# Encoder layer on one core: token-major projections with weights taken 512 columns at a time instead of 256

## The chip, the cores and the metric

The kernel runs on 1 core of one Trainium2 chip. The metric is the device time of one execution in microseconds (us); before the change it is 2485.04 us, the median of 3 runs (2484.7 to 2485.36).

## The reference, cut to what matters

One encoder layer is applied to two independent streams: a prompt of 1024 tokens and a sample of 512 tokens, each with a memory of 256 tokens, width 1024, everything float32.

```python
def encoder_layer(x, mem, p):
    u = rmsnorm(x, p['mix_norm_g']) @ p['w_in']
    ssd_out = ssd_mixer(u[..., OFF_Z:OFF_XBC], u[..., OFF_XBC:OFF_DT], u[..., OFF_DT:OFF_Q], ...)
    att_out = attention_mixer(u[..., OFF_Q:OFF_K], u[..., OFF_K:OFF_V], u[..., OFF_V:IN_COLS], ...)
    h = x + jnp.concatenate([ssd_out, att_out], axis=-1).astype(x.dtype) @ p['w_out']
    h = h + memory_cross_attention(rmsnorm(h, p['xatt_norm_g']), rmsnorm(mem, p['mem_norm_g']), ...)
    hm = rmsnorm(h, p['mlp_norm_g'])
    return h + jnp.square(jax.nn.relu(hm @ p['mlp_w1'])) @ p['mlp_w2']
```

`w_in` gives in turn the gates (512 columns), the convolved channels (1024), the step sizes (16), queries, keys and values (512 each). The memory projection `xatt_wkv` has 2048 columns, `w_out` 1024.

## The kernel before, in words

**Products.** A float32 product is made of three float32r products: operand = high part + low part, and `mm3` (lines 198 to 201) adds high x high, high x low and low x high in one PSUM bank. `load_w` (line 179) brings 1 MB of weights: four DMAs of 256 KB into `raw` (4 buffers), four ScalarE casts to `whi` (line 189), four subtractions to `wlo` (line 191), in turns on GpSimd and VectorE. `whi` and `wlo` have three buffers each.

**Token-major projections.** Gates, queries, keys, values, memory keys and values, and the output projection are computed with a tile of 128 tokens stationary and weights moving. `slab` takes 256 columns of all 1024 rows; `proj` (line 273) makes 24 products of 256 columns for one token tile into one of three `mm` banks:

```python
        for k in range(KT):
            mm3(ps, hi[:, k, ts], lo[:, k, ts], wh[:, k, :], wl[:, k, :], k == 0, k == KT - 1)
```

What reads the bank: for gates a tanh on ScalarE and a product on VectorE (lines 381, 382); for queries and keys a ScalarE copy (line 511), then `heads` (norm and rotation on ScalarE, VectorE and GpSimd) and, one pair of tiles later, `transposed`; for memory keys a copy and a square (lines 896, 898), and right behind them scaling (line 910) and TensorE transposes (line 912); for memory values a copy, a cast on VectorE (line 901) and a subtraction on GpSimd (line 902); for the output projection an addition to the residual on VectorE (line 958).

**Other dense work.** `xbc` (the convolved channels) and the feed-forward (`mlp`) already move 512 columns per product; the cross-attention queries move 256 and stay so.

**The order.** Every dense part is a generator that yields after about 3 us of TensorE work. `weave` advances the mixers (`ssd`, the scan, and `att`, the dilated attention, first of the sample, then of the prompt) by a rate of steps per yield, and side work (norms and transposes of tokens) by another. A tile scheduler then fixes each engine's order when the program is built; engines run their orders strictly and wait on semaphores. In time the program runs: sample `w_in` (0 to 91 us), its gates (to 111), its queries, keys, values (to 197), prompt gates (to 256), prompt `xbc` (to 380), prompt queries, keys, values (to 572), memory (to 725), sample output projection (to 790), sample cross-attention (to 960), sample feed-forward (to 1415), prompt output projection (to 1515), prompt cross-attention (to 1760), prompt feed-forward (to the end).

Of the kernel before, what the change touches and what calls it, by code (L numbers as in the profile page):

```python
# [84 lines left out]
def encoder(ctx: ExitStack, tc: tile.TileContext, I, y_p, y_s):  # L85
# [186 lines left out]
    def proj(w, quads, t):  # L272
# [6 lines left out]
        return ps  # L279

# [19 lines left out]
    def w_in(st, pool, wx, first=False):  # L300
# [67 lines left out]
        def gates(b):  # L368
            for c in range(2):
                if b == 0:  # L370
                    wz.append(slab(W_IN, OFF_Z + c * 256))
                yield from gate(c, wz[c], range(b * 4, b * 4 + 4, 2))

        def gate(c, w, ts):
            for t in ts:
                th = pool.tile([128, 512], F32, name="ev").rearrange("p (t c) -> p t c", t=2)
                for i in range(2):
                    if i:
                        yield
                    ps = proj(w, at, t + i)  # L380
                    nc.scalar.activation(th[:, i], ps, AF.Tanh, scale=0.5)
                    nc.vector.scalar_tensor_tensor(th[:, i], th[:, i], 1.0, ps, op0=OP.add, op1=OP.mult)  # L382
                dst = st.zs[t * 128:t * 128 + 256, c * 256:c * 256 + 256]
                nc.sync.dma_start(dst.rearrange("(t p) c -> p t c", p=128), th)
                catch_up()
                yield
# [64 lines left out]
    def w_in_qkv(st, pool, rot, mid=None):  # L451
# [7 lines left out]
        def heads(c, t, hl):  # L459

            qk = c // 2
            e, sq = f(hl[1]).rearrange("p (t c) -> p t c", t=2), f(hl[0])
            x = e.rearrange("p t (h e) -> p t h e", h=4)
            x3 = e.rearrange("p t (h e) -> p (t h) e", h=4)
            nc.scalar.activation(sq, e.rearrange("p t c -> p (t c)"), AF.Square)
# [3 lines left out]
            nc.vector.tensor_tensor(x3, x3, r[:, :8, None].to_broadcast([128, 8, 64]), op=OP.mult)  # L469
            t1, t2 = x[..., 0:8], x[..., 8:16]  # L470
            m = sq[:, 0:256].rearrange("p (j t h c) -> p j t h c", j=4, t=2, h=4)
            for j, src in enumerate((t1, t2, t1, t2)):
                w = rot[qk][:, t:t + 2, j, None, :].to_broadcast([128, 2, 4, 8])
# [4 lines left out]
        def transposed(c, t, hl):  # L478
            qk = c // 2
            e = f(hl[1]).rearrange("p (t c) -> p t c", t=2)  # L480
            pt = tp_bank()
            for hp in range(2):
                for i in range(2):
                    o = (hp * 2 + i) * 128
                    nc.tensor.transpose(pt[:, o:o + 128], e[:, i, hp * 128:hp * 128 + 128], perm)
# [3 lines left out]
            for j in range(2):  # L489
                dst = st.qk[qk, (c % 2) * 2:(c % 2) * 2 + 2, j, :, t * 128:t * 128 + 256]  # L490
                nc.sync.dma_start(dst.rearrange("h p t -> p h t"), f(hl[j]).rearrange("p (h t) -> p h t", h=2))
# [3 lines left out]
        order = [(c, t) for c in range(4) for t in range(0, nt, 2)]  # L495
        order += [(c, b * 4 + t) for b in range(nt // 4) for c in (4, 5) for t in (0, 2)]
        ws = {}
        for c, t in order:
            if c not in ws:
                ws[c] = slab(W_IN, OFF_Q + c * 256)  # L500
            w = ws[c]
            if mid and (c, t) == (4, 4):
                mid()
            if True:
                hl = [pool.tile([128, 512], F32R, name="ev") for _ in range(2 if c < 4 else 1)]
                e = f(hl[-1]).rearrange("p (t c) -> p t c", t=2)
                for i in range(2):
                    if i:
                        yield
                    ps = proj(w, st.at, t + i)  # L510
                    nc.scalar.copy(e[:, i], ps)
                if behind:
                    transposed(*behind.pop())
                if c < 4:
                    heads(c, t, hl)
                    behind.append((c, t, hl))
                else:
                    for i in range(2):
# [4 lines left out]
                yield  # L523
# [359 lines left out]
    def memory(pool, late=None):  # L883
        for c in range(8):
            w = slab(WKV, c * 256)
            if late and c == 4:
                late()
            for st in (S, R):
                need("mem" + st.tag)
                kf = pool.tile([128, 512], F32, name="ev").rearrange("p (m c) -> p m c", m=2)  # L890
                ss = pool.tile([128, 2], F32, name="kss", bufs=2)
                for mt in range(2):
                    if mt:
                        yield
                    ps = proj(w, st.mt[:1], st.mt[1] + mt)
                    nc.scalar.copy(kf[:, mt], ps)
                    if c < 4:
                        nc.scalar.activation(ps, ps, AF.Square, accum_out=ss[:, mt:mt + 1])
                hl = [pool.tile([128, 2, 256], F32R, name="ev") for _ in range(2)]
                if c >= 4:  # L900
                    nc.vector.tensor_copy(hl[0], kf)
                    nc.gpsimd.tensor_tensor(hl[1], kf, f(hl[0]), op=OP.subtract)
                    for j in range(2):
                        nc.sync.dma_start(st.v[:, c - 4, j], f(hl[j]).rearrange("p m c -> p (m c)"))
                    yield
                    continue
                r = rstd(pool, ss, 2, 256)
                pt = tp_bank().rearrange("p (e m) -> p e m", e=2)
                for mt in range(2):
                    nc.vector.tensor_scalar(kf[:, mt], kf[:, mt], r[:, mt:mt + 1], None, op0=OP.mult)  # L910
                    for e in range(2):
                        nc.tensor.transpose(pt[:, e, mt * 128:mt * 128 + 128], kf[:, mt, e * 128:e * 128 + 128], ident)
# [347 lines left out]
```

## Time and profile before

| | |
|---|---|
| median of 3 runs | 2485.04 us |
| the profiled execution | 2483.99 us |
| its span (first to last instruction) | 2481.9 us |
| TensorE products busy | 2413.2 us, 97% of the span, 14435 |
| VectorE, ScalarE, GpSimd busy | 57%, 39%, 30% |
| granted TensorE clock, mean | 0.986 |
| DMA | 272.28 MB, 35.2% of 16 engines |

TensorE products overlap in the pipeline and their ends are modelled, so the busy share says only that the engine seldom stands still. What one product costs is read from the distance between the starts of two that follow each other. A wait is shown in brackets in the timeline: how long the engine stood, and what released it.

### The profile page before, as it was taken

What the parts mean: (1) busy time and instruction counts of PE and PEld (TensorE: products, weight loads), DVE (VectorE), ACT (ScalarE), POOL (GpSimd) and SP (SyncE); (2) the same over time, 40 slices, a digit from 0 to 9 for tenths busy, and PEclk for the clock granted to TensorE, in tenths of its full rate; (3) what the DMA queues carried; (4) which work ended last, traced back from release to release, by engine and by line L of the source; (5) the groups of instructions that cost most, each with busy time, mean ns of one, the idle gap of its engine ahead of it and who ended that gap; (6) DMA issues with size and microseconds to landing.
All of it is one profiled execution on the core that took longest, in us unless ns stands there. A gap on an engine that the chain in (4) does not pass through costs nothing.

```text
span 2481.9 us, 38736 instructions
## 1 busy us (share of the span) xinstructions
PE 2413.2 (97%) x14435; PEld 2129.5 (86%) x14435; DVE 1416.4 (57%) x2870; ACT 977.0 (39%) x2393; POOL 749.0 (30%) x612
## 2 busy tenths in 40 slices
PE   8899999999899998999999999999999999999999
PEld 6899789998798997888888899999888888888887
DVE  7676876658866566565655636555634434444344
ACT  6445455545544555444433325333521211212111
POOL 3253313425654212332424212111222222322221
PEclk9999999999899999999999999999999999999999
DMA  5555344547675344335335511111111111111111
GB/s 182 182 191 172 121 138 144 169 135 256 226 256 161 87 124 117 105 107 134 107 95 179 181 45 50 54 52 52 35 44 42 52 52 34 54 49 51 51 34 68
DMA packets 258603, 272.28 MB, mean 110 GB/s; under 512 B 43474, under 2 KB 222960, under 8 KB 258416
## 3 DMA queue, kind: packets, MB, share of 16 engines
q1 hardware_dynamic: 258416, 269.82, 35.2%
q8 instruction: 114, 1.87, 0.3%
q14 instruction: 73, 0.60, 0.1%
HBM read 215.55 MB, written 54.20 MB: 109 GB/s over the span
## 4 chain that ended last, share of the span: by engine, by line
PE 73%; DMA 3%; DVE 3%; issue 1%; ACT 1%; POOL 1%; SPq 0%; ACTq 0%; POOLq 0%; DVEq 0%
PE mm L199 15%; PE mm L201 14%; PE mm L200 14%; PE tp L199 7%; PE tp L200 7%; PE tp L201 7%; PE mc L800 2%; PE ma L771 1%; PE mb L787 1%; PE tp L218 1%; DMA se<-acp 1%; DVE se L626 1%; PE mc L635 0%; DMA ak<-qkp 0%; PE tp L981 0%
## 5 line engine op out<-in xcount | busy, mean ns | idle before, releaser
L191 POOL TENSOR_TENSOR wlo<-raw,whi 128x512 fp32r<-128x512 f32 x240 | 364.9, 1537 | 550.3 <-ACT whi L189 451.2
L199 PE MATMUL mm<-whi,chi 128*128 128x256 f32 x1792 | 521.1, 292 | 2.3 <-DVE ev L382 1.7
L201 PE MATMUL mm<-whi,clo 128*128 128x256 f32 x1792 | 511.6, 288 | 1.3 <-DVE clo L225 1.2
L200 PE MATMUL mm<-wlo,chi 128*128 128x256 f32 x1792 | 511.6, 286 | 0.0
L1112 DVE TENSOR_TENSOR h<-mm,h 128x512 f32<-128x512 f32 x384 | 262.5, 688 | 380.7 <-PE mm L201 380.4
L191 DVE TENSOR_TENSOR wlo<-raw,whi 128x512 fp32r<-128x512 f32 x240 | 296.7, 1250 | 97.1 <-ACT whi L189 96.2
L199 PEld LDWEIGHTS mm<-whi,chi 128*128 128x128 f32 x1792 | 344.6, 192 | 5.0 <-DVE ev L382 2.4
L189 ACT CAST whi<-raw 128x512 fp32r<-128x512 f32 x480 | 265.2, 618 | 203.8 <-PE tp L200 100.3
L200 PEld LDWEIGHTS mm<-wlo,chi 128*128 128x128 f32 x1792 | 344.3, 192 | 0.8
L201 PEld LDWEIGHTS mm<-whi,clo 128*128 128x128 f32 x1792 | 342.2, 192 | 2.3 <-DVE clo L225 2.2
L199 PE MATMUL mm<-whi,hidh 128*128 128x512 f32 x768 | 304.2, 396 | 0.0
L201 PE MATMUL mm<-whi,hidl 128*128 128x512 f32 x768 | 303.1, 395 | 0.0
L200 PE MATMUL mm<-wlo,hidh 128*128 128x512 f32 x768 | 302.6, 394 | 0.0
L200 PE MATMUL tp<-clo,whi 128*128 128x512 f32 x720 | 284.4, 395 | 0.0
L199 PE MATMUL tp<-chi,whi 128*128 128x512 f32 x720 | 284.3, 395 | 0.0
L201 PE MATMUL tp<-chi,wlo 128*128 128x512 f32 x720 | 284.0, 394 | 0.0
L1096 POOL TENSOR_TENSOR hidl<-hr,hidh 128x512 fp32r<-128x512 f32 x96 | 124.6, 1298 | 475.7 <-ACT hidh L1095 302.6
L1095 ACT CAST hidh<-hr 128x512 fp32r<-128x512 f32 x96 | 59.6, 621 | 401.1 <-PE mm L200 325.7
L201 PEld LDWEIGHTS mm<-whi,hidl 128*128 128x128 f32 x768 | 144.4, 188 | 33.6
L200 PEld LDWEIGHTS mm<-wlo,hidh 128*128 128x128 f32 x768 | 144.6, 188 | 32.3
L199 PEld LDWEIGHTS mm<-whi,hidh 128*128 128x128 f32 x768 | 144.5, 188 | 32.2
L201 PEld LDWEIGHTS tp<-chi,wlo 128*128 128x128 f32 x720 | 135.4, 188 | 31.1
(284 smaller groups left out, 4132.7 us busy)
## 6 DMA issues: line engine op xcount, KB each, us to landing
raw<-in_mlp_w_dram SPq DMA_DIRECT2D x256, 256.0 KB
raw<-in_w_in_dram SPq DMA_DIRECT2D x96, 256.0 KB
qkp<-ev SPq DMA_DIRECT2D x32, 256.0 KB
raw<-in_xatt_wkv_dram SPq DMA_DIRECT2D x32, 256.0 KB
se<-acp SPq DMA_DIRECT2D x16, 512.0 KB
raw<-in_w_out_dram SPq DMA_DIRECT2D x32, 256.0 KB
raw<-in_xatt_wq_dram SPq DMA_DIRECT2D x32, 256.0 KB
ak<-qkp SPq DMA_DIRECT2D x32, 256.0 KB
```

The source lines that it names most:

```text
L189: nc.scalar.copy(hi[:, sl, sc], raw)
L191: eng.tensor_tensor(lo[:, sl, sc], raw, f(hi[:, sl, sc]), op=OP.subtract)
L199: nc.tensor.matmul(ps, lh, rh, start=start, stop=False)
L200: nc.tensor.matmul(ps, lh, rl, start=False, stop=False)
L201: nc.tensor.matmul(ps, ll, rh, start=False, stop=stop)
L218: nc.tensor.transpose(pt[:, k, t, :], xn[t][:, (2 * kp + k) * 128:(2 * kp + k + 1) * 128], units(2 * kp + k))
L626: nc.vector.scalar_tensor_tensor(w[:, h], cbm[:, 0, g], col[2], w[:, h], op0=OP.mult, op1=OP.add)
L771: nc.tensor.matmul(pq[:, i, :W], qu, ops[i][0][j], start=j == 0, stop=j == 1)
L800: nc.tensor.matmul(po[:, i * 64:i * 64 + 64], pT[:, i * nk + j, :], ops[i][1][j][:, rs], start=j == 0, stop=j == nk - 1)
L1095: nc.scalar.copy(hh[:, ft], r)
L1096: nc.gpsimd.tensor_tensor(hl[:, ft], r, f(hh[:, ft]), op=OP.subtract)
L1112: nc.vector.tensor_tensor(h[t][:, cs], ps, h[t][:, cs], op=OP.add)
```

## The change

Weights of the token-major projections come as two halves of 512 rows with 512 columns each (`wide_slab`), 1 MB per half, so one wide slab holds two of the three weight buffers. `wide_proj` takes token tiles in pairs with a bank each: both tiles on one half, then both on the other, and the next pair begins with the half used last. What reads a bank now reads 512 columns at once; memory keys are finished one head later through a list `behind`; memory values lose the copy on ScalarE and VectorE's cast (a ScalarE cast and a VectorE subtraction straight from the bank remain), and GpSimd's subtraction goes. DMA rows change with it: weights 2 KB instead of 1 KB, gates and values 2 KB instead of 1 KB, queries and keys 512 bytes instead of 1 KB. The rates of `weave` change too. A yield still stands for about the same work: 12 products of 512 columns instead of 24 of 256.

```diff
+        r, c = {8: (2, 256), 4: (1, 512), 2: (2, 256)}[a]
         for s in range(4):
-            raw = wp.tile([128, 2, 256], F32, name="raw", bufs=4)
-            sl = slice(s * 2, s * 2 + 2) if a == 8 else slice(0, 2)
-            sc = slice(0, 256) if a == 8 else slice(s * 256, s * 256 + 256)
+            raw = wp.tile([128, 512], F32, name="raw", bufs=4).rearrange("p (r c) -> p r c", r=r)
+            sl = slice(s * r, s * r + r) if a > 2 else slice(0, 2)
+            sc = slice(0, c) if a > 2 else slice(s * c, s * c + c)
...
+    def wide_slab(w, c0):
+        src = w[:, c0:c0 + 512].rearrange("(u k p) c -> u p k c", p=128, k=4)
+        return [load_w(src[u], 4, 512) for u in range(2)], [0]
...
+    def wide_proj(w, quads, tiles, each):
+        halves, last = w
+        for t0 in tiles[::2]:
+            ps = [mm_bank() for _ in range(2)]
+            for n in range(2):
+                u = last[0] if n == 0 else 1 - last[0]
+                wh, wl = halves[u]
+                for i in range(2):
+                    hi, lo = quads[(t0 + i) // 4]
+                    ts = slice((t0 + i) % 4 * 128, (t0 + i) % 4 * 128 + 128)
+                    for k in range(4):
+                        kk = u * 4 + k
+                        mm3(ps[i], hi[:, kk, ts], lo[:, kk, ts], wh[:, k, :], wl[:, k, :],
+                            n == 0 and k == 0, n == 1 and k == 3)
+                    if n == 1:
+                        each(t0 + i, ps[i])
+                    yield
+            last[0] = 1 - last[0]
...
+            if b == 0:
+                wz.append(wide_slab(W_IN, OFF_Z))
+            yield from wide_proj(wz[0], at, range(b * 4, b * 4 + 4), gate)
+        def gate(t, ps):
+            th = pool.tile([128, 512], F32, name="ev")
+            nc.scalar.activation(th, ps, AF.Tanh, scale=0.5)
+            nc.vector.scalar_tensor_tensor(th, th, 1.0, ps, op0=OP.add, op1=OP.mult)
+            nc.sync.dma_start(st.zs[t * 128:t * 128 + 128, :], th)
+            catch_up()
...
+        def query_key(qk):
+            def each(t, ps):
+                hl = [pool.tile([128, 512], F32R, name="ev") for _ in range(2)]
+                nc.scalar.copy(f(hl[1]), ps)
                 if behind:
                     transposed(*behind.pop())
-                if c < 4:
-                    heads(c, t, hl)
-                    behind.append((c, t, hl))
-                else:
-                    for i in range(2):
-                        for g in range(2):
-                            r0 = 64 + (t + i) * 128 + g * 64
-                            dst = st.vd[r0:r0 + 64, (c - 4) * 256:(c - 3) * 256]
-                            nc.sync.dma_start(dst.rearrange("(r j) c -> j r c", r=4), e[g * 64:g * 64 + 64, i, :])
-                yield
+                heads(qk, t, hl)
+                behind.append((qk, t, hl))
+            return each
+        def value(t, ps):
+            e = pool.tile([128, 512], F32, name="ev")
+            nc.scalar.copy(e, ps)
+            if behind:
+                transposed(*behind.pop())
+            for g in range(2):
+                r0 = 64 + t * 128 + g * 64
+                dst = st.vd[r0:r0 + 64, :]
...
+        for part, each in enumerate((query_key(0), query_key(1), value)):
+            w = wide_slab(W_IN, OFF_Q + part * 512)
+            for b in range(nt // 4):
+                if mid and part == 2 and b == 1:
+                    mid()
+                yield from wide_proj(w, st.at, range(b * 4, b * 4 + 4), each)
...
+        def values(st, c, t, ps):
+            hl = [pool.tile([128, 512], F32R, name="ev") for _ in range(2)]
+            nc.scalar.copy(hl[0], ps)
+            nc.vector.tensor_tensor(hl[1], ps, f(hl[0]), op=OP.subtract)
+            for j in range(2):
+                dst = st.v[:, c:c + 2, j, t % 2 * 256:t % 2 * 256 + 256]
+                nc.sync.dma_start(dst, f(hl[j]).rearrange("p (h c) -> p h c", h=2))
+        behind = []
+        for c in range(4):
...
+                        behind.extend(held)
+                    for _ in range(len(behind) - 1):
+                        keys(*behind.pop(0))
+                yield from wide_proj(w, st.mt[:1], range(st.mt[1], st.mt[1] + 2), each)
...
+        def each(t, ps):
+            hs = st.h[t][:, cs]
             nc.vector.tensor_tensor(hs, ps, hs, op=OP.add)
-            if c == 3 and t % 2:
+            if cs.start and t % 2:
                 done(t // 2)
-            yield
+        for c in range(2):
+            w = wide_slab(W_OUT, c * 512)
+            cs = slice(c * 512, c * 512 + 512)
+            for pr in range(st.nt // 2):
+                need("mix%d%s" % (pr, st.tag))
+                yield from wide_proj(w, st.mixT, range(pr * 2, pr * 2 + 2), each)
...
-        weave(mixing, 0.3, marked(w_in_qkv(S, pool, rot), "qkv s"))
+        weave(mixing, 0.4, marked(w_in_qkv(S, pool, rot), "qkv s"))
-        weave(mixing, 0.45, marked(w_in(R, pool, wx), "w_in p"), 1.0)
+        weave(mixing, 0.5, marked(w_in(R, pool, wx), "w_in p"), 1.0)
-        weave(mixing, 0.9, marked(w_in_qkv(R, pool, rot, memories), "qkv p"), 1.0)
+        weave(mixing, 1.0, marked(w_in_qkv(R, pool, rot, memories), "qkv p"), 1.0)
-        weave(mixing, 0.6, chain(S, (atA,), hp, tp_only), 2.0)
+        weave(mixing, 0.7, chain(S, (atA,), hp, tp_only), 2.0)
-            weave(mixing, 0.65, mlp(S, hid, ready))
+            weave(mixing, 0.5, mlp(S, hid, ready))
```

The change also moves instructions. **TensorE, sample gates and queries:** `ma<-sxs,sbt` is the scan's first state update (line 582 before, 594 after); `mm<-w..,chi/clo` are gate and query products. Before:

```order
L201 MATMUL mm<-whi,clo 128x256
L549 MATMUL ma<-ident,sacs 64x128
L582 MATMUL ma<-sxs,sbt 128x256 x2
L199 MATMUL mm<-whi,chi 128x256
L200 MATMUL mm<-wlo,chi 128x256
```

Now:

```order
L206 MATMUL mm<-wlo,chi 128x512
L207 MATMUL mm<-whi,clo 128x512
L594 MATMUL ma<-sxs,sbt 128x256 x2
L205 MATMUL mm<-whi,chi 128x512
L206 MATMUL mm<-wlo,chi 128x512
```

Before, the update stands behind the third of the eight gate projections (72 of 192 products); now it stands behind all 96 wide gate products and the first 96 wide products of the queries.

**TensorE, end of the prompt gates:** `tp<-ident,xn` transposes normalised tokens of the second block of the prompt, `mc`, `mb`, `ma` belong to the scan. Before:

```order
L201 MATMUL mm<-whi,clo 128x256
L635 MATMUL mc<-sx,se 128x64 x4
L199 MATMUL mm<-whi,chi 128x256
L200 MATMUL mm<-wlo,chi 128x256
L199 MATMUL mm<-whi,chi 128x256
L200 MATMUL mm<-wlo,chi 128x256
L201 MATMUL mm<-whi,clo 128x256 x2
L635 MATMUL mc<-sx,se 128x64 x2
L199 MATMUL mm<-whi,chi 128x256
L200 MATMUL mm<-wlo,chi 128x256
L199 MATMUL mm<-whi,chi 128x256
L200 MATMUL mm<-wlo,chi 128x256
```

Now:

```order
L594 MATMUL ma<-sxs,sbt 128x256
L224 MATMUL tp<-ident,xn 128x128 x2
L594 MATMUL ma<-sxs,sbt 128x256
L647 MATMUL mc<-sx,se 128x64 x5
L224 MATMUL tp<-ident,xn 128x128 x6
L647 MATMUL mc<-sx,se 128x64 x3
L619 MATMUL mb<-sbc 128x128 x2
L656 MATMUL ma<-carry,sbc 128x256 x2
L656 MATMUL mb<-spb,sbc 128x256 x2
L224 MATMUL tp<-ident,xn 128x128 x8
L594 MATMUL ma<-sxs,sbt 128x256 x2
L205 MATMUL mm<-whi,chi 128x512
```

Before, gate products stand between the small ones; now 34 small instructions follow each other with no gate product between them.

## Rows read from the trace of the kernel before

**Rows 1.** The page: engines' busy time, and the TensorE clock in 40 slices.

```profile
PE 2413.2 (97%) x14435; PEld 2129.5 (86%) x14435; DVE 1416.4 (57%) x2870; ACT 977.0 (39%) x2393; POOL 749.0 (30%) x612
...
PEclk9999999999899999999999999999999999999999
```

**Rows 2.** Busy time by stretch, the page's engines in columns, clock, DMA.

```profile
core 0: us, PE busy (x) PEld busy (x) DVE busy (x) ACT busy (x) POOL busy (x), PEclk, DMA share, GB/s
...
91.00:111.00 20.00, 20.00 (x144) 20.00 (x145) 10.46 (x19) 9.66 (x23) 6.19 (x6) 0.85 0.72 231
...
572.00:725.00 153.00, 138.27 (x1015) 131.85 (x1014) 124.25 (x242) 84.75 (x246) 91.86 (x74) 0.93 0.70 231
...
1850.00:2400.00 550.00, 550.00 (x2370) 445.40 (x2369) 223.92 (x295) 110.75 (x196) 142.08 (x98) 1.00 0.15 48
```

**Rows 3.** Groups by line and shape: busy us, mean ns, idle before.

```profile
L199 PE MATMUL mm<-whi,chi 128*128 128x256 f32 x1792 | 521.1, 292 | 2.3 <-DVE ev L382 1.7 <-ACT chi L224 0.4
L200 PE MATMUL mm<-wlo,chi 128*128 128x256 f32 x1792 | 511.6, 286 | 0.0
```

**Rows 4.** Timeline of TensorE, prompt memory values: start, duration.

```profile
694.38 0.28 PE L201 MATMUL mm<-whi,clo 128*128 128x256 f32 x1
...
696.52 0.29 PE L201 MATMUL mm<-whi,clo 128*128 128x256 f32 x1
```

**Rows 5.** Timeline of TensorE, sample gates.

```profile
87.20 2.04 PE L582 MATMUL ma<-sxs,sbt 128*128 128x256 f32 x4 [5.32 <-DMA sbt<-bts]
90.97 0.58 PE L199 MATMUL mm<-whi,chi 128*128 128x256 f32 x1 [1.73 <-DVE ev L382]
91.36 0.42 PE L200 MATMUL mm<-wlo,chi 128*128 128x256 f32 x1
...
96.69 0.41 PE L201 MATMUL mm<-whi,clo 128*128 128x256 f32 x1
...
97.98 0.28 PE L201 MATMUL mm<-whi,clo 128*128 128x256 f32 x1
```

**Rows 6.** Waits of TensorE: total us, times, longest.

```profile
PE mc L635 <- POOL se L628: 9.7, 4, 4.3
PE tp L218 <- DVE xn L239: 8.9, 7, 4.5
PE tp L218 <- DVE clo L225: 8.6, 3, 3.4
...
PE tp L912 <- DVE ev L910: 3.0, 3, 1.1
```

**Rows 7.** Timeline, one slab made in the memory stage.

```profile
637.28 2.18 ACT L189 CAST whi<-raw 128x512 fp32r<-128x512 f32 x4 [2.58 <-PE mm L201]
638.46 3.06 DVE L191 TENSOR_TENSOR wlo<-raw,whi 128x512 fp32r<-128x512 f32 x2 [1.45 <-ACT whi L189]
```

**Rows 8.** Timeline, a slab made where the output projection begins.

```profile
723.80 0.28 PE L201 MATMUL mm<-whi,clo 128*128 128x256 f32 x1
730.55 2.18 ACT L189 CAST whi<-raw 128x512 fp32r<-128x512 f32 x4
...
736.89 1.27 POOL L191 TENSOR_TENSOR wlo<-raw,whi 128x512 fp32r<-128x512 f32 x1
```

**Rows 9.** Groups by line and shape: what reads the banks.

```profile
L1112 DVE TENSOR_TENSOR h<-mm,h 128x512 f32<-128x512 f32 x384 | 262.5, 688 | 380.7 <-PE mm L201 380.4
...
L511 ACT COPY ev<-mm 128x256 f32<-128x256 f32 x72 | 26.0, 368 | 41.6 <-PE mm L201 36.0 <-DMA qks<-ev 3.3 <-DMA vds<-ev 2.0
L958 DVE TENSOR_TENSOR h<-mm,h 128x256 f32<-128x256 f32 x48 | 20.0, 421 | 38.1 <-PE mm L201 38.0
...
L336 ACT COPY xr<-mm 128x512 f32<-128x512 f32 x24 | 13.9, 580 | 19.6 <-PE mm L201 15.0 <-DVE cacc L348 4.6
L902 POOL TENSOR_TENSOR ev<-ev 128x512 fp32r<-128x512 f32 x8 | 11.8, 1481 | 11.5 <-DVE ev L901 8.5 <-issue 2.3 <-POOL wlo L191 0.7
```

More of the change, by code (lines that the diff above doesn't have):

```diff
@@ L489, in transposed @@
             for j in range(2):
-                dst = st.qk[qk, (c % 2) * 2:(c % 2) * 2 + 2, j, :, t * 128:t * 128 + 256]
-                nc.sync.dma_start(dst.rearrange("h p t -> p h t"), f(hl[j]).rearrange("p (h t) -> p h t", h=2))
+                dst = st.qk[qk, :, j, :, t * 128:t * 128 + 128]
+                nc.sync.dma_start(dst.rearrange("h p t -> p h t"), f(hl[j]).rearrange("p (h t) -> p h t", h=4))
         behind = []
-        order = [(c, t) for c in range(4) for t in range(0, nt, 2)]
@@ L496, in w_in_qkv @@
[L496 to L511, printed above, removed]
+        def query_key(qk):
+            def each(t, ps):
+                hl = [pool.tile([128, 512], F32R, name="ev") for _ in range(2)]
+                nc.scalar.copy(f(hl[1]), ps)
@@ L523, in w_in_qkv @@
-                yield
+                heads(qk, t, hl)
[9 more added lines that the diff above has]
+                dst = st.vd[r0:r0 + 64, :]
+                nc.sync.dma_start(dst.rearrange("(r j) c -> j r c", r=4), e[g * 64:g * 64 + 64, :])
@@ L883, in memory, with keys @@
     def memory(pool, late=None):
-        for c in range(8):
-            w = slab(WKV, c * 256)
-            if late and c == 4:
+        def keys(st, c, kf, ss):
+            hl = [pool.tile([128, 2, 256], F32R, name="ev") for _ in range(2)]
+            r = rstd(pool, ss, 2, 256)
+            pt = tp_bank().rearrange("p (e m) -> p e m", e=2)
+            for mt in range(2):
+                nc.vector.tensor_scalar(kf[:, mt], kf[:, mt], r[:, mt:mt + 1], None, op0=OP.mult)
+                for e in range(2):
+                    nc.tensor.transpose(pt[:, e, mt * 128:mt * 128 + 128], kf[:, mt, e * 128:e * 128 + 128], ident)
+            for e in range(2):
+                g = gqk[:, e:e + 1]
+                nc.scalar.activation(hl[0][:, e], pt[:, e], AF.Identity, scale=g)
+                nc.vector.scalar_tensor_tensor(hl[1][:, e], pt[:, e], g, f(hl[0][:, e]), op0=OP.mult, op1=OP.subtract)
+            for j in range(2):
+                nc.sync.dma_start(st.kt[:, c, j], f(hl[j]).rearrange("p e m -> p (e m)"))
+        def values(st, c, t, ps):
+            hl = [pool.tile([128, 512], F32R, name="ev") for _ in range(2)]
+            nc.scalar.copy(hl[0], ps)
+            nc.vector.tensor_tensor(hl[1], ps, f(hl[0]), op=OP.subtract)
+            for j in range(2):
+                dst = st.v[:, c:c + 2, j, t % 2 * 256:t % 2 * 256 + 256]
+                nc.sync.dma_start(dst, f(hl[j]).rearrange("p (h c) -> p h c", h=2))
+        behind = []
+        for c in range(4):
+            w = wide_slab(WKV, c * 512)
+            if late and c == 2:
                 late()
@@ L899, in memory @@
[L899 to L908, printed above, removed]
@@ L917, in memory @@
-                for j in range(2):
-                    nc.sync.dma_start(st.kt[:, c, j], f(hl[j]).rearrange("p e m -> p (e m)"))
-                yield
+                held = []
+                def each(t, ps):
+                    if c > 1:
+                        if behind:
+                            keys(*behind.pop(0))
+                        return values(st, c * 2 - 4, t, ps)
+                    mt = t % 2
+                    for h in range(2):
+                        if mt == 0:
+                            kf = pool.tile([128, 512], F32, name="ev").rearrange("p (m c) -> p m c", m=2)
+                            held.append((st, c * 2 + h, kf, pool.tile([128, 2], F32, name="kss", bufs=6)))
+                        _, _, kf, ss = held[h]
+                        cs = slice(h * 256, h * 256 + 256)
+                        nc.scalar.copy(kf[:, mt], ps[:, cs])
+                        nc.scalar.activation(ps[:, cs], ps[:, cs], AF.Square, accum_out=ss[:, mt:mt + 1])
+                    if mt:
+                        behind.extend(held)
+                    for _ in range(len(behind) - 1):
+                        keys(*behind.pop(0))
@@ L946, in w_out, with each @@
             st.h.append(x)
-        ws = {}
-        order = [(c, t) for c in range(2) for t in range(st.nt)]
-        order += [(c, pr * 2 + t) for pr in range(st.nt // 2) for c in (2, 3) for t in range(2)]
-        for c, t in order:
-            if c not in ws:
-                ws[c] = slab(W_OUT, c * 256)
-            if c == 0 and t % 2 == 0:
-                need("mix%d%s" % (t // 2, st.tag))
-            ps = proj(ws[c], st.mixT, t)
-            hs = st.h[t][:, c * 256:c * 256 + 256]
+        def each(t, ps):
+            hs = st.h[t][:, cs]
             nc.vector.tensor_tensor(hs, ps, hs, op=OP.add)
-            if c == 3 and t % 2:
+            if cs.start and t % 2:
                 done(t // 2)
-            yield
+        for c in range(2):
[4 more added lines that the diff above has]
+                yield from wide_proj(w, st.mixT, range(pr * 2, pr * 2 + 2), each)
     def xattn(st, xk, xp, bank, done):
```

58 lines of the change are left out of this document (11 added, 47 removed).

## The prediction

> **What bounds the kernel now.** I read first the page's engine rows: TensorE is busy for 97% of the span, no other engine for more than 57% [rows 1]. The reader should see that time is to be won or lost only on TensorE's own line: in the distance between its products, in its waits, and in its clock. That share says nothing of distance, because products overlap: one of 256 columns is shown as 292 ns long [rows 3] while the next starts 0.119 us later [rows 4]. So the second view is the timeline: from 694.38 to 696.52 lie 18 steps, 2.14 us / 18 = 0.119 us per product of 256 columns [rows 4]. For 512 columns I use the stretch 1850 to 2400, where the prompt's feed-forward moves only 512-column products and TensorE never stands: 550 us / 2370 = 0.232 us [rows 2]. The third view is the list of TensorE's waits: some ten us each for four kinds [rows 6], all in the first 970 us, where scan, attention and norms run beside the projections. The fourth is the clock: it falls in a few slices only [rows 1], and the timeline shows when: after a wait of 5.3 and one of 1.7 us, products start 0.213 us apart for 25 steps (91.36 to 96.69), half clock (1.2 GHz), before 0.12 comes back [rows 5]. In the windows the memory stage is the worst: TensorE idle for 14.7 of 153 us at clock 0.93, VectorE busy for 124.25 [rows 2].
>
> **The change part by part.** The sum is made against the profiled execution's 2483.99 us; the median of the runs is 1.05 us above it.
>
> *Fewer, wider products.* 5376 products of 256 columns run on lines 199 to 201 (1792 on each, [rows 3]); the cross-attention queries keep 1152 of them (4 slabs x 12 tiles x 24). The other 4224 become 2112 of 512 columns. Each pair cost 2 x 0.119 = 0.238 us and becomes 0.232 us [rows 2, 4]: 0.0057 us x 2112 = 12.0 us off. All of it is on TensorE's line. Bounds: one stretch of 18 steps is read to about 0.01 us, so 0.1194 is as possible, which makes 14 us; and at half clock, where 256 columns take 0.213 [rows 5], no row shows 512 columns, so nothing is counted there. I take 12, bounds 5 and 17. The Trainium skill, "TensorE: Matmul & The Clock Gate", section "Back-to-back issue gap", speaks against a gain of this size: it gives a lone gap of N/2.4 + 2.5 ns, so that a merged pair saves only 2.5 ns, an estimate of 5.3 us for 2112. The rows are above its gaps at both widths (119 against 109, 232 against 216), and the measurement decides.
>
> *The scan's first update in the sample's gates.* Before, it stands behind the third gate projection and waits 5.32 us for a load; VectorE, standing behind the same update, then reads a gate bank late, another 1.73 us; 25 products follow at half clock, 25 x (0.213 - 0.119) = 2.4 us [rows 4, 5]. Together 9.4 us. Now it stands behind all 96 wide gate products and 96 of the queries, 192 x 0.232 = 44.5 us after the gates begin, where before it stood 72 x 0.119 = 8.6 us after: 36 us later, against a load that came 5.3 us late. I take all 9.4; bounds 0 (another wait comes there) and 9.4.
>
> *The cluster at the end of the prompt's gates.* Now 34 small instructions of scan and norm follow each other without gate products between. They are chained through VectorE, ScalarE and GpSimd, as the scan's and the norm's known waits are [rows 6]. The nearest price is a wait of the norm for VectorE's low part, 8.6 us in 3 times, 2.9 each, plus half clock as in [rows 5], 2.4: I take 5. Bounds 0 and 12 (the longest norm wait, 4.5, and the longest scan wait, 4.3 [rows 6], with half clock after).
>
> *Memory keys one head later.* Their transposes waited 3.0 us in 3 times for the scaling [rows 6]; with a head's delay I take 2 off, bounds 0 and 3.
>
> *Halves of weights.* A second half finds its buffer only when the previous slab's half is left. From there to its first use lie at least the second tile's other half (12 products) and the next pair on the first half (24): 36 x 0.232 = 8.4 us, where a whole spare slab stood before. How long does making a slab take after the release? 4.2 us in the memory stage: ScalarE stood ready and cast at 637.28, VectorE ended at 641.52 [rows 7]. At the output projection's start 14.1 us: the last product that read the buffer ended at 724.08, the casts began at 730.55 and GpSimd ended at 738.16 [rows 8]. So a wait is between 0 and 5.7 us. Most stages are like the first, so I take 2 us in all. Queued behind such casts on ScalarE are copies out of banks; TensorE needs the first of those banks again only 24 products later.
>
> *Priced at nothing.* Bank readers: VectorE's 48 additions of 421 ns become 24 of 688, ScalarE's 72 copies of 368 ns become 36 of 580 [rows 9]; both lie beside TensorE's work, and would cost only where these engines are late already. GpSimd loses 8 x 1.48 us of memory values [rows 9]; the 9.7 us that TensorE waited for GpSimd [rows 6] could shrink by it, but the removed work stands later than those waits, so: nothing, bound 9.7 off. Banks: a pair holds two of three; from the end of its first tile to the need of that bank lie 24 wide products, 5.6 us, as before two projections, 5.7. DMA: the same bytes, in longer rows for weights and shorter for queries and keys; its share is 0.70 at most in these stages [rows 2]. Rates: a yield stands for the same work, so 0.1 more only moves scan and attention forward, out of the sample's feed-forward; their products cost the same there. The cover is VectorE's idle time, least in the memory stage (28.75 of 153 us, [rows 2]), whose rate stays.
>
> Sum: -12.0 - 9.4 + 5 - 2 + 2 = -16.4 us; 2483.99 - 16.4 = 2467.6, and with the 1.05 us of the median 2469 rounded.
>
> **The rivals.**
> *Paid back (no change).* Wide products save only some 2.5 ns per pair, the wait at the sample's gates goes, and the prompt's cluster (12) and halves (6) take the place: -5 - 9.4 + 12 - 2 + 2 = -2.4 to 2483. For it: that scheduled orders always leave some such waits, and that the fixed part of 5.7 ns is a small difference of two readings. Against it: 2370 products agree on 0.232. The skill's gap from above would make the first term 5.3 instead of 12.
>
> *Memory loosens (larger gain).* Its scan no longer waits for GpSimd (9.7 and 3.0 us, [rows 6]), with half clock after them (clock 0.93 of 153 us is 21 us at half speed, 10.7 lost, [rows 2]): 20 of these come off: 2449. For: 11.8 us less on GpSimd. Against: VectorE is busy for 81% there, and stays so.
>
> *Halves late (slower).* In the built order eight of the sixteen second halves have only 8 to 13 us of products between release and first use (at 0.232 us each), 10.4 on average. If making one takes 14.1 us [rows 8] in all of these, they wait 8 x 3.7 = 30 us together, and some five of them long enough for half clock as in [rows 5], 12 us more: 2469 - 2 + 42 = 2509. It decides from about 12 us per half on, where the gain is gone. For: VectorE and GpSimd carry the subtractions and are busiest in these stages. Against: [rows 7], and the four casts wait at the head of ScalarE's queue as they do now.
>
> That the change doesn't do what it says is excluded: the built order has 2112 products of 512 columns where 4224 of 256 stood.
>
> **How the numbers follow.** About 0.2% (5 us) is what a measurement of this kernel can tell from no change. Forecast 0.63 (2455 to 2480), paid back 0.13, memory loosens 0.13, halves late 0.11. Faster takes forecast and memory: 0.76; same 0.13; slower 0.11. The range leaves out halves late and the far half of memory loosens: 2447 to 2489; its ends are also the bounds of the terms (-17 - 9.4 - 9.7 - 3 = -39 below, -5 + 12 + 6 - 9.4 = +4 above).
>
> **What would show it.** Right: products on 512 columns start 0.232 us apart in gates, queries, keys, values, memory and output projection; no wait for `sbt` around 85 us and full clock through the sample's gates; prompt gates longer by some us with a wait of the norm or scan there. Waits for `whi` or `wlo` at 8 us or less of products would show the halves. Wrong: a distance of 0.238 or more, or more waits in memory and output projection than before, or a change of the sample feed-forward's length by more than the attention steps it loses.

## The result, and the profile after

The changed kernel takes 2456.31 us, the median of 4 runs (2454.34 to 2459.82), beside 2485.2 us for the kernel before: ratio 0.9886, 95% interval 0.9868 to 0.9903. It is faster by 28.9 us, inside the range on record and 12.7 us below the number forecast. The profiled execution took 2455.78 us with a span of 2454.0.

The page of the kernel after, engines and TensorE clock:

```profile
PE 2393.4 (98%) x12323; PEld 2005.8 (82%) x12323; DVE 1410.0 (57%) x2834; ACT 967.3 (39%) x2337; POOL 736.3 (30%) x604
...
PEclk9999999999989999999999999999999999999999
```

Against [rows 1] there are 2112 TensorE products fewer; one slice of 40 is under nine tenths of full clock in either, and the mean granted clock is 0.993 (0.986 before). The other engines do nearly the same work. The groups by shape, then a piece of the timeline inside the sample's gates:

```profile
L205 PE MATMUL mm<-whi,chi 128*128 128x512 f32 x704 | 288.2, 409 | 8.8 <-ACT chi L230 5.6 <-ACT ev L513 2.3 <-ACT mm L942 0.8
...
L205 PE MATMUL mm<-whi,chi 128*128 128x256 f32 x384 | 108.9, 285 | 0.0
```

```profile
85.06 0.40 PE L207 MATMUL mm<-whi,clo 128*128 128x512 f32 x1
...
89.23 0.39 PE L207 MATMUL mm<-whi,clo 128*128 128x512 f32 x1
89.47 0.53 PE L549 MATMUL mb<-sa,tab 128*128 128x32 f32 x4
89.83 0.41 PE L550 MATMUL mb<-sa,one 128*128 128x64 f32 x2
90.05 0.48 PE L205 MATMUL mm<-whi,chi 128*128 128x512 f32 x1
```

From 85.06 to 89.23 lie 18 steps: 4.17 / 18 = 0.232 us, the distance forecast. There is no idle time in brackets where [rows 5] had 5.32 and 1.73 us. TensorE's longest kinds of waits over the whole span, after its wait for the program's first load:

```profile
PE mm L205 <- ACT chi L230: 5.6, 3, 2.7
PE ma L656 <- DVE carry L601: 5.2, 3, 3.8
PE tp L224 <- DVE clo L231: 4.7, 2, 3.3
PE mc L647 <- POOL se L640: 4.7, 4, 2.3
...
PE tp L903 <- DVE ev L901: 2.0, 3, 0.8
```

Against [rows 6], the waits for GpSimd's `se` fell from 9.7 to 4.7 us and the memory keys' wait from 3.0 to 2.0; no wait is put down to `whi` or `wlo`. The stages from memory to the sample's feed-forward, four before and then four after, cut where the same share of the weight products is done (columns as in [rows 2]):

```profile
567.00:725.00 158.00, 143.04 (x1050) 136.31 (x1050) 128.99 (x252) 88.41 (x255) 94.10 (x76) 0.94 0.72 236
725.00:787.00 62.00, 57.86 (x460) 56.69 (x458) 45.96 (x91) 26.82 (x66) 31.84 (x25) 0.97 0.57 187
787.00:972.00 185.00, 172.32 (x1216) 160.11 (x1217) 119.11 (x306) 103.66 (x297) 42.90 (x38) 0.95 0.45 121
972.00:1411.00 439.00, 437.88 (x2262) 368.37 (x2262) 254.92 (x529) 182.27 (x447) 152.10 (x105) 1.00 0.42 124
```

```profile
542.00:718.00 176.00, 153.40 (x718) 122.40 (x717) 146.61 (x290) 96.45 (x275) 92.64 (x77) 0.94 0.73 238
718.00:775.00 57.00, 55.18 (x268) 45.23 (x266) 33.73 (x75) 23.59 (x58) 20.94 (x18) 0.97 0.78 234
775.00:972.00 197.00, 189.73 (x1405) 177.71 (x1404) 129.72 (x374) 118.58 (x362) 44.34 (x38) 0.98 0.46 122
972.00:1387.00 415.00, 413.05 (x2038) 343.43 (x2037) 242.29 (x438) 160.31 (x370) 154.47 (x104) 1.00 0.39 119
```

The memory stage became 18 us longer, with TensorE idle for 22.6 us instead of 15. The cross-attention stage became 12 us longer at a better clock, and the feed-forward shorter (972 to 1411 before, 439 us; now 415). Part of that is work moved forward: the memory stage holds 257 of the scan's products (208 before), cross-attention 520 of attention's (340), the feed-forward 460 (684). Of the memory stage's 18 us, though, 11.7 are lost time, by the account below.

To tell moved work from lost time, one account was made of every kernel here. For each kind of TensorE product (tiles and columns) take the median distance from its start to the next start in each kernel, and of these the smallest. Their sum over all products is the *work*; what the distances hold beyond it is *lost*: idle time, and the half clock's extra. The 7 to 8 us before the first product are counted as work. Stages are cut at the same share of weight products done. In us:

| kernel | work | lost | sample gates | sample q,k,v and prompt input | prompt q,k,v | memory | sample out and cross-att. | other |
|---|---|---|---|---|---|---|---|---|
| before | 2378.5 | 98.4 | 11.3 | 12.2 | 5.9 | 26.5 | 28.0 | 14.5 |
| e1 | 2378.2 | 99.1 | 9.3 | 13.9 | 7.0 | 25.4 | 27.6 | 15.8 |
| e2 | 2378.6 | 94.4 | 10.8 | 8.5 | 9.6 | 35.4 | 16.8 | 13.4 |
| e5 | 2376.3 | 88.9 | 0.0 | 16.2 | 3.2 | 26.9 | 29.9 | 12.8 |
| e3 | 2364.1 | 101.1 | 0.0 | 16.5 | 2.6 | 33.0 | 30.3 | 18.8 |
| e7 | 2364.2 | 99.5 | 0.0 | 17.0 | 2.9 | 34.2 | 30.8 | 14.8 |
| e11 | 2364.0 | 92.3 | 0.0 | 14.4 | -0.1 | 32.9 | 31.4 | 13.7 |
| e9 | 2363.9 | 90.6 | 0.0 | 14.7 | 0.0 | 21.3 | 41.4 | 13.1 |
| e4 | 2364.1 | 84.9 | 0.0 | 7.9 | 3.4 | 34.5 | 25.4 | 13.7 |
| **after** | 2364.8 | 84.4 | 0.0 | 11.9 | 1.9 | 38.2 | 16.9 | 15.5 |
| e6 | 2366.6 | 88.1 | 0.0 | 9.8 | 1.7 | 36.4 | 24.2 | 16.0 |
| e8 | 2363.9 | 85.7 | 0.0 | 14.1 | 2.3 | 36.7 | 18.2 | 14.3 |
| e12 | 2363.9 | 79.1 | 0.0 | 10.3 | -0.7 | 26.7 | 25.8 | 17.0 |
| e10 | 2364.1 | 75.5 | 0.0 | 14.1 | -0.6 | 28.0 | 19.8 | 14.2 |

Between before and after, work fell by 13.7 us and lost time by 14.0. The sample's gates alone lost 11.3 before and nothing after. The account is one execution per kernel; its sums follow the medians to a few us. By it the sample's gates begin at 71.5 us, earlier than the list of stages ahead of the prediction has them.

### The profile page after: what moved, and what is told of

It reads as the page before. It is cut to its first block, busy times and chain, and to the rows that moved or that the text cites. A ratio compares the mean times of both kernels' runs of the same rounds, so it can differ in the third digit from the quotient of the medians.

```text
span 2454.0 us, 34361 instructions
## 1 busy us (share of the span) xinstructions
PE 2393.4 (98%) x12323; PEld 2005.8 (82%) x12323; DVE 1410.0 (57%) x2834; ACT 967.3 (39%) x2337; POOL 736.3 (30%) x604
## 4 chain that ended last, share of the span: by engine, by line
PE 78%; DMA 6%; DVE 5%; ACT 1%; issue 1%; SPq 1%; POOL 0%; ACTq 0%; DVEq 0%; POOLq 0%
PE mm L205 16%; PE mm L206 16%; PE mm L207 16%; PE tp L205 7%; PE tp L207 7%; PE tp L206 7%; PE mc L812 3%; PE ma L783 2%; DMA se<-acp 1%; PE mb L799 1%; DVE wlo L192 1%; PE tp L224 1%; DVE se L636 1%; DMA se<-acs 1%; DVE se L638 1%
## 5 line engine op out<-in xcount | busy, mean ns | idle before, releaser
L205 PE MATMUL mm<-whi,chi 128*128 128x512 f32 (+1 forms) x1088 | 397.1, 366 | 8.8 <-ACT chi L230 5.6
L206 PE MATMUL mm<-wlo,chi 128*128 128x512 f32 (+1 forms) x1088 | 392.2, 361 | 0.0
L207 PE MATMUL mm<-whi,clo 128*128 128x512 f32 (+1 forms) x1088 | 392.1, 363 | 0.0
L205 PEld LDWEIGHTS mm<-whi,chi 128*128 128x128 f32 x1088 | 207.1, 190 | 39.2 <-ACT chi L230 7.0
L207 PEld LDWEIGHTS mm<-whi,clo 128*128 128x128 f32 x1088 | 206.5, 190 | 28.6
L206 PEld LDWEIGHTS mm<-wlo,chi 128*128 128x128 f32 x1088 | 206.9, 190 | 27.5
```

Source lines behind the costliest of these rows:

```text
L205: nc.tensor.matmul(ps, lh, rh, start=start, stop=False)
L206: nc.tensor.matmul(ps, lh, rl, start=False, stop=False)
L207: nc.tensor.matmul(ps, ll, rh, start=False, stop=stop)
```

## The experiments

The kernel before took 2482.6 to 2484.8 us beside them (medians).

**e1: is it the scan's first update?** The prediction put the loss in the sample's gates down to that update and the load it waits for. Here a zero, worked out from the first pair of queries, is added to an input of the sample's scan, so that the update cannot stand in the gates.

```diff
+                    if st is S and c == 0 and t == 0 and i == 1:
+                        nc.vector.tensor_scalar(late0, f(e)[:, 1, 0:1], 0.0, None, op0=OP.mult)
...
+        if st is S:
+            nc.vector.tensor_scalar(dd, dd, late0, None, op0=OP.add)
```

> The kernel before, with one change: the scan of the sample reads one number more (a zero made from the first pair of query projections), so its first state update cannot stand among the sample's gates; in the built order it now stands 15 projections later. Theory (a wait of 5.3 us for a load, a late bank of 1.7 us and half clock after both were lost there): the gap at 82 to 91 us goes, full clock through the gates, 2485 - 9 = 2476 us, give or take 4. Rival (the order has no slack and the wait comes back elsewhere): 2483 to 2488.

Measured: 2483.91 us, ratio 0.9997 (0.9988 to 1.0007): no gain. TensorE, in the timeline of e1, and VectorE beside it:

```profile
82.69 0.27 PE L554 MATMUL ma<-ident,sacs 128*64 128x128 f32 x1
89.97 0.58 PE L200 MATMUL mm<-whi,chi 128*128 128x256 f32 x1 [7.00 <-DVE ev L383]
90.34 0.41 PE L201 MATMUL mm<-wlo,chi 128*128 128x256 f32 x1
```

```profile
85.07 0.75 DVE L349 SCALAR_TENSOR_TENSOR cacc<-xr,halfc,cacc 128x512 f32<-128x512 f32 x1 [1.90 <-ACT cacc L347]
85.74 0.22 DVE L546 TENSOR_TENSOR sdd<-sdd,dts 128x64 f32<-128x64 f32 x1
85.87 2.32 DVE L349 SCALAR_TENSOR_TENSOR cacc<-xr,halfc,cacc 128x512 f32<-128x512 f32 x3
...
89.50 1.08 DVE L383 SCALAR_TENSOR_TENSOR ev<-ev,mm 128x256 f32<-128x256 f32 x3
```

The fourth narrow gate projection wants the first of three banks back. That bank's reader (line 383, line 382 in the kernel before) stands on VectorE behind the last of the convolution (`cacc`) and runs at 89.50. Before, the scan's update and its late load only filled the same 7 us (5.32 + 1.73): with the update gone, TensorE waits just as long for the bank, and half clock follows again (0.21 us between starts until 94.6). The theory fell. The new one: in the changed kernel the first bank is wanted back later, and that took the wait away.

**e5: wide gates alone.** The kernel before with `wide_slab`, `wide_proj` and the new `gates` and `gate`; everything else narrow, the rates as before.

```diff
         def gates(b):
-            for c in range(2):
-                if b == 0:
-                    wz.append(slab(W_IN, OFF_Z + c * 256))
-                yield from gate(c, wz[c], range(b * 4, b * 4 + 4, 2))
+            if b == 0:
+                wz.append(wide_slab(W_IN, OFF_Z))
+            yield from wide_proj(wz[0], at, range(b * 4, b * 4 + 4), gate)
```

> The kernel before with only the gates taken 512 columns wide, by pairs of tiles (288 wide products in place of 576); all else is narrow as before. Theory (three banks: the fourth narrow gate projection comes back to the first bank 8.6 us after the gates begin, while its reader stands behind VectorE's convolution work; by pairs the first bank is wanted again only after 60 wide products, 13.9 us): the wait of 5 to 7 us at 85 to 90 us and the half clock after it are gone, 9.4 us, and 288 x 0.0057 = 1.6 us of streaming: about 2474, less up to 5 us that the prompt's gates may give back, so 2474 to 2479. Rival (the wait only moves to the queries, as it moved when the scan alone was put later): within 3 us of before, 2482 to 2485.

Measured: 2472.63 us, ratio 0.9952 (0.9936 to 0.9969), 10.0 us under the kernel before in medians and 11.9 by the ratio. The gates' window, e5:

```profile
70.00:94.00 24.00, 24.00 (x113) 19.64 (x112) 18.38 (x34) 11.37 (x22) 4.86 (x4) 1.00 0.62 197
```

The same stretch of the kernel before, where TensorE was idle for 7 of 24 us:

```profile
72.00:96.00 24.00, 16.95 (x112) 15.81 (x111) 18.09 (x39) 11.83 (x29) 5.37 (x4) 0.81 0.76 231
```

VectorE is no earlier for it: its first bank reader runs 17.4 us after the first gate product in e5 (70.14 to 87.49) and 16.9 in e1 (72.61 to 89.50). VectorE in e5, and TensorE where the fourth tile begins:

```profile
86.88 0.69 DVE L379 SCALAR_TENSOR_TENSOR cacc<-ev,cacc 128x512 f32<-128x512 f32 x1 [0.56 <-ACT ev L378]
87.49 1.28 DVE L404 SCALAR_TENSOR_TENSOR ev<-ev,mm 128x512 f32<-128x512 f32 x2
```

```profile
87.52 0.39 PE L207 MATMUL mm<-whi,clo 128*128 128x512 f32 x1
87.75 0.53 PE L557 MATMUL mb<-sa,tab 128*128 128x32 f32 x4
88.11 0.41 PE L558 MATMUL mb<-sa,one 128*128 128x64 f32 x2
88.34 0.48 PE L205 MATMUL mm<-whi,chi 128*128 128x512 f32 x1
```

What changed is when TensorE wants the bank: after the first pair (48 wide products) the built order runs all 24 of the third tile, which has the third bank, before the fourth tile. That is 72 x 0.232 = 16.7 us of products ahead of the return to the first bank, where 72 x 0.119 = 8.6 us stood before. The fourth tile begins at 88.34 (at 90.05 in the kernel after), just behind its reader, so the wait is gone by a small margin. The number of products ahead of the return is 72 in either kernel; what grew is the length of each. That pairs of tiles add anything to the 512 columns was not tested. The Trainium skill, "Perfetto Trace Analysis", section "Matmuls", advises rotating independent products through banks so that emptying one overlaps the next; e1 and e5 agree and add that three banks are enough only if the products between cover the reader's lateness, here some 7 us.

**e4: halves without turns.** The kernel after, but each pair of tiles begins with the first half.

```diff
-            last[0] = 1 - last[0]
```

> The changed kernel, where every pair of tiles takes the first half of rows first (no turns). The last half used is then always the second, so a new slab's second half may be loaded 12 to 24 products (3 to 6 us) earlier. Theory (in the trace after, every half is ready 2.4 us or more before its first product, so halves cost nothing): 2456 give or take 5. Rival (late halves hold TensorE up through ScalarE's queue): faster by 5 us or more, 2451 or less. A third: turns save something in the order, slower by 5 or more.

Measured: 2457.01 us, ratio 0.9886 (0.987 to 0.9903), the same as after. The order of the halves neither gains nor costs anything that shows, though the built order changed with it (225 of the scan's products in the memory stage, 257 in the kernel after).

**e6: the memory stage as before.** The kernel after with `memory` narrow (8 slabs of 256 columns, one tile at a time).

```diff
-        for c in range(4):
-            w = wide_slab(WKV, c * 512)
+        for c in range(8):
+            w = slab(WKV, c * 256)
...
-                yield from wide_proj(w, st.mt[:1], range(st.mt[1], st.mt[1] + 2), each)
+                    ps = proj(w, st.mt[:1], st.mt[1] + mt)
```

> The kernel after with the memory stage as it was before (256 columns, one tile at a time, keys without the head's delay); all else wide, same rates. Theory (the wide memory stage costs and gains nothing but its streaming; its longer waits come from scan work that the rates moved into it): 384 x 0.0057 = 2.2 us slower, about 2458.5. Rival (pairs of tiles and keys in fours hold TensorE up there: idle and slow time rose from 26 to 38 us): 12 - 2 = 10 us faster, about 2446.

Measured: 2460.95 us, ratio 0.9907 (0.9883 to 0.9932): 4.6 us over the kernel after, with overlapping intervals. The stage lost 36.4 us narrow and 38.2 wide, so its own wide products do not make its greater loss. Two other kernels show how far that can be taken: the kernel before with the new rates (e2) loses 35.4 there instead of 26.5, but the wide kernel with the old rates (e3) loses 33.0. The number of the scan's products in the stage does not set the loss either: 216 in e2, 199 in e3, and 231 in e10, which loses 28.0. Its cause stays open.

**e2 and e3: the five rates.** e2 is the kernel before with the new rates, e3 the kernel after with the old ones:

```diff
-        weave(mixing, 0.4, marked(w_in_qkv(S, pool, rot), "qkv s"))
+        weave(mixing, 0.3, marked(w_in_qkv(S, pool, rot), "qkv s"))
...
-        weave(mixing, 0.5, marked(w_in(R, pool, wx), "w_in p"), 1.0)
+        weave(mixing, 0.45, marked(w_in(R, pool, wx), "w_in p"), 1.0)
...
-        weave(mixing, 1.0, marked(w_in_qkv(R, pool, rot, memories), "qkv p"), 1.0)
+        weave(mixing, 0.9, marked(w_in_qkv(R, pool, rot, memories), "qkv p"), 1.0)
...
-        weave(mixing, 0.7, chain(S, (atA,), hp, tp_only), 2.0)
+        weave(mixing, 0.6, chain(S, (atA,), hp, tp_only), 2.0)
...
-            weave(mixing, 0.5, mlp(S, hid, ready))
+            weave(mixing, 0.65, mlp(S, hid, ready))
```

> The kernel before with the five new rates of weave alone. Theory (rates only move attention and scan to earlier stages): 2485 give or take 5, the 5.3 us wait in the sample's gates unchanged. Rival (the part of the gain beyond streaming and the scan's wait, some 8 us, is made by the rates, which put attention into idle time of TensorE before the feed-forward): 2477 or less.

> The changed kernel with the five old rates. Theory: 2456 give or take 5. Rival (rates make some 8 us): 2464 or more.

Measured: e2 2481.29 us (0.9987, 0.9977 to 0.9998), e3 2476.56 us (0.9967, 0.9952 to 0.9982). In the narrow kernel the rates bring 3 us, in the wide one 20. The wide kernel with the old rates gives back more than half of its 25 us of streaming and gates (13.7 + 11.3): outside the gates it loses 101.1 us where the kernel before loses 98.4 - 11.3 = 87.1, and the 14 us more are spread over prompt input, memory and the rest. Why wide products and the old rates lose them together is not shown.

**e7 and e8: which rates.** The three early rates of that diff set back (e7), or the two late ones (e8).

> The kernel after with the three early rates of before (queries and keys of the sample 0.3, prompt's input 0.45, prompt's queries and keys 0.9), the two late rates as after. All five old rates together cost 20 us. Theory (what counts is how much attention is left when the sample's feed-forward begins, since TensorE never waits there and each attention step costs its full length): the early rates leave the scan and so the attention later, and with the feed-forward's rate of 0.5 it isn't made up; about half of the 20 us, 2463 to 2469. Rival (only the late pair matters): 2455 to 2458.

> The kernel after with the two late rates of before (sample's output projection and cross-attention 0.6, its feed-forward 0.65), the three early rates as after. Theory (attention left for the feed-forward costs its full length): 0.1 less per step of the output projection and cross-attention leaves more attention for the feed-forward; about half of the 20 us, 2463 to 2469. Rival (only the early rates matter): 2455 to 2458.

Measured: e7 2472.23 us (0.9955, 0.9939 to 0.997), e8 2456.36 us (0.9891, 0.9876 to 0.9907). The early ones make 16 us, the late ones nothing, though e8 has 72 more attention products than the kernel after in the feed-forward: what is left for that stage is not the cause, against the theory of both; e8's rival held. In e7 the scan is late: 80 of its products stand behind the start of the sample's output projection, 16 in the kernel after, and TensorE waits there for them (waits of e7 in 700 to 785 us):

```profile
PE mc L647 <- POOL se L640: 5.3, 3, 3.8
PE ma L594 <- DVE syo L658: 2.4, 1, 2.4
PE ma L656 <- DVE carry L601: 2.4, 1, 2.4
```

**e9, e10, e11: one rate at a time, and further.** If the late scan is what costs, its amount should set the time.

```diff
-        weave(mixing, 0.4, marked(w_in_qkv(S, pool, rot), "qkv s"))
+        weave(mixing, 0.3, marked(w_in_qkv(S, pool, rot), "qkv s"))
```

> The kernel after with one early rate of before: the sample's queries and keys at 0.3 in place of 0.4. In the built order 54 of the scan's 202 groups of products then still stand behind the start of the sample's output projection (8 in the kernel after, 40 with the three old early rates, which cost 16 us). Theory (what costs is the prompt's scan that runs on beside the output projection and the cross-attention, where TensorE has too little else to do): 2468 to 2476. Rival (the 16 us came from the waits in the prompt's gates or from the prompt's queries and keys at 0.9): 2455 to 2462.

```diff
-        weave(mixing, 1.0, marked(w_in_qkv(R, pool, rot, memories), "qkv p"), 1.0)
+        weave(mixing, 0.9, marked(w_in_qkv(R, pool, rot, memories), "qkv p"), 1.0)
```

> The kernel after with one early rate of before: the prompt's queries and keys at 0.9 in place of 1.0. Up to that stage the order is the kernel's own; 24 of the 202 groups of the scan stand behind the start of the sample's output projection (8 in the kernel after). Theory (the scan that is left costs): 2457 to 2464. Rival (this rate alone makes the 16 us): 2468 to 2473.

```diff
-        weave(mixing, 0.4, marked(w_in_qkv(S, pool, rot), "qkv s"))
+        weave(mixing, 0.5, marked(w_in_qkv(S, pool, rot), "qkv s"))
...
-        weave(mixing, 0.5, marked(w_in(R, pool, wx), "w_in p"), 1.0)
+        weave(mixing, 0.6, marked(w_in(R, pool, wx), "w_in p"), 1.0)
```

> The kernel after with two early rates raised further: the sample's queries and keys 0.5 (0.4), the prompt's input 0.6 (0.5). In the built order the whole scan stands ahead of the sample's output projection, and the sample's attention begins in the prompt's input products. Theory (the scan left behind costs): no scan wait in the output projection and some less in memory, 2446 to 2455. Rival (the scan has to wait for its own chain of small steps wherever it stands, and the waits only move forward): 2455 to 2462.

Measured: e9 2459.6 us (0.9904, 0.9872 to 0.9935), e10 2444.96 us (0.9838, 0.9818 to 0.9859), e11 2462.19 us (0.9909, 0.989 to 0.9929). All three miss the theory; only e9 is where its rival put it. e9 has the most of the scan left of all (108 products) and loses 41.4 us beside the output projection and cross-attention, but only 21.3 in memory, so the time barely moves. e11 has none left, and loses as much there as e7 (31.4, 30.8), where 664 of attention's products now stand (564 in the kernel after). e10 leaves 48 and is the fastest of all. The memory stage of e10, with 231 of the scan's products:

```profile
540.00:701.00 161.00, 144.39 (x689) 117.26 (x688) 135.36 (x269) 89.44 (x255) 89.45 (x72) 0.95 0.78 249
```

TensorE is idle for 16.6 us of it, not 22.6.

**e12: a neighbour of e10.** The same rate at 0.92.

```diff
-        weave(mixing, 1.0, marked(w_in_qkv(R, pool, rot, memories), "qkv p"), 1.0)
+        weave(mixing, 0.92, marked(w_in_qkv(R, pool, rot, memories), "qkv p"), 1.0)
```

> The kernel after with the prompt's queries and keys at 0.92, a nudge beside the 0.9 that made it 11 us faster than the kernel after. Theory (the last 15 us either way are how the few late steps happen to fall in one built order, and no rule of the rate): it need not follow its neighbour, anywhere from 2445 to 2462. Rival (a slightly lower rate there is better in itself, since less of the scan stands in the memory stage): 2444 to 2449.

Measured: 2447.54 us, ratio 0.9846 (0.9823 to 0.9868). The neighbour agrees, but it is a near one: the scan's products stand as in e10, 231 in the memory stage and 48 behind it. With 0.3 and 0.45 beside it the same 0.9 belongs to a kernel 27 us slower (e7). Over the wide kernels the sum of what memory, output projection and cross-attention lose goes roughly with the time (47.8 in e10, 52.5 in e12, 54.9 in e8, 55.1 after, 59.9 in e4, 62.7 to 65.0 in e9, e11, e3 and e7), but e3 and e7 lose 7 to 9 us more in all than e11 at nearly the same sum. That the scan's chain makes TensorE wait wherever it stands, and that the rates set how much other work stands with it, fits the waits of e7 and is not shown. Why a given set of rates loses less is not settled, and 0.45 alone was not tried.

## Why the prediction was right, and where it was not

- *Fewer, wider products*, 12.0 us forecast: right. Work fell by 13.7 us, 0.0065 us per pair instead of 0.0057; e5's 288 products gave 2.2. The estimate of 5.3 us from the Trainium skill's lone gap ("TensorE: Matmul & The Clock Gate", "Back-to-back issue gap") does not hold for these streams of products.
- *The scan's first update in the sample's gates*, 9.4 us forecast: the size held (11.3 lost before, 0 after), the cause did not. e1 took the update away and gained nothing; the wait belonged to the bank's late reader. That the size held was luck: the reader's wait was as long as the load's. The step that failed is the sentence under *Priced at nothing* that banks stay as they were, 5.6 us against 5.7. It counted from the end of the bank's own products, as if the reader could begin there; but the reader stood on VectorE behind the convolution, and began 16.9 us after the first gate product in e1 and 17.3 in the kernel after, so what counted was how long after that beginning the bank is wanted again: 16.7 us of wide products, 8.6 of narrow ones.
- *The cluster at the end of the prompt's gates*, 5 us: right in sign, somewhat large. By the account, cut at both ends of the prompt's gates, they lost 4.8 us before and 8.3 after, 3.5 more: TensorE waits 1.56 us at 225 and 2.52 at 230, with half clock to 237, where before it waited 2.08 at 220. The sample's queries, keys and values and the prompt's `xbc` lost less in turn (4.9 to 3.2 and 2.6 to 0.5), so the column of the table shows nothing of it (12.2 and 11.9).
- *Memory keys one head later*, 2 us off: 3.0 to 2.0 in the waits. Half the size, and small beside the 11.7 us more that the stage loses.
- *Halves of weights*, 2 us: nothing. No wait for `whi` or `wlo` appears in the kernel after, and e4 changed the turns without effect. The rival *halves late* is out.
- *Rates*, nothing: the largest miss. Without them the wide kernel is at 2476.56, where the other terms should have given 2469: wide products at the old rates lose 14 us more outside the gates. With them 20 us come off. The argument that a yield stands for the same work held for work (2364 to 2365 us in every kernel that is wide throughout) and not for lost time.
- The rival *memory loosens* was right that the waits for GpSimd shrink (9.7 to 4.7) and wrong about the stage, which loses more. The work taken off GpSimd is not what shrinks them: e2, where GpSimd still has it, waits 0.8 us in all, and e4, where it is gone, 9.0 (the waits of e2, then of e4; before, 9.7 [rows 6]):

```profile
PE mc L635 <- POOL se L628: 0.8, 1, 0.8
```

```profile
PE mc L646 <- POOL se L639: 9.0, 6, 3.3
```

Of the signs of being wrong one came, more waits in the memory stage, beside a result in the range. Two readings in the prediction are slightly off and change nothing: the DMA share reaches 0.72, not 0.70 [rows 2], and the lower bounds, -39 us, end at 2446, not 2447.

So the sign came from two terms that were sound in size, one of them for the wrong reason. The 12.7 us between forecast and result are two effects that the sum had at nothing: the wide kernel with the old rates is 7.6 us above the forecast, and the rates take off 20.3. That they end inside the range was not foreseen.

## What to carry to other kernels

Before crediting an edit with removing a wait, ask what TensorE would wait for next at the same place: a late load can stand in front of a late bank reader of the same length, and only the second has to go. Count how many products lie before a bank is wanted again, in the built order, against the lateness of its reader: 72 products of 512 columns in place of 72 of 256 bought 8 us here without any engine being faster. And where a rate of interleaving is changed with an edit, price it by itself: rates alone moved this wide kernel between 2445 and 2477 us, and setting one of the five back (0.9 for the prompt's queries and keys) beats both kernels, by 11 us the one after.

## What the runs showed of the hardware that was not expected

At half clock a merged pair saves nothing. The prediction had no row for 512 columns there; the kernel after has, behind the wait at 230 us:

```profile
234.25 0.63 PE L206 MATMUL mm<-clo,whi 128*128 128x512 f32 x1
...
236.39 0.63 PE L205 MATMUL mm<-chi,whi 128*128 128x512 f32 x1
```

```profile
234.00:236.50 2.50, 2.50 (x8) 1.94 (x7) 2.50 (x7) 2.50 (x8) 1.28 (x1) 0.50 0.03 13
```

Five steps take 2.14 us, 0.428 each at a granted clock of 0.50 (1.2 GHz), which is about twice the 0.213 of 256 columns [rows 5]. In these rows the 6 ns per pair exist only at full clock, where 0.232 stands against 2 x 0.119.
